# An arena of on-chip places for a streaming encoder step: a new order of handing places out, and two column pairs moved

## The chip, the core and the metric

The kernel runs on one core of a Trainium2 chip. The metric is the device time of one execution in microseconds (us), less being better. Engines are named as the profile names them: PE multiplies matrices and PEld loads its weights, DVE, ACT and POOL work on vectors, SP and POOL (and here and there ACT) issue transfers (DMAs). Each engine works through its own instructions in the order in which the program gives them.

## What is computed

One layer of a hybrid encoder, for 512 rows of a new stream and 32 rows of a running one (544 rows in all, width 2048), everything in fp32:

```python
mod = silu(c) @ w_ada + b_ada                       # shift, scale, gate
h = rmsnorm(x, norm_g) * (1 + scale) + shift
z = h @ w_in                                        # 120 blocks of 128 columns
ya = gelu(au) * (tril(ws) @ rmsnorm(gelu(av)) + bs) * silu(ag)      # 8 groups
yb = rglru(causal_conv(lx)) * silu(lg)                              # 8 blocks
yc = rmsnorm(hgrn2_scan(hq, hf, hi)) * silu(hg)                     # 8 heads
out = (ga * (ya @ wb0) + gb * (yb @ wb1) + gc * (yc @ wb2)) @ w_out # ga, gb, gc: sigmoid(mg)
y = rmsnorm(x + gate * out, final_g)
```

The states of the recurrences and the normalised rows of `av` are outputs too.

## The kernel before

**Stages.** First comes the conditioning and `h` (about the first 130 us). Then the 120 column blocks of `w_in` are multiplied in 60 pairs of columns, one `Group` each; then the three branch products (`merges`), then `w_out` and the final norm. Each matrix product is done with an operand split into a high and a low part, three matmuls for each 128x128 weight block.

**A group.** The rows are cut in two halves of 272 (`HF`), and two column blocks are done in seven products ("items") of 24 matmuls each, in the order `2, 6, -1, 5, -7, 3, 4`, where -1 and -7 are items 1 and 7 of the group that follows. The last group has no group after it, so its items are 2, 6, 5, 3, 4. Items 6, 5 and 3 of a group add up in the same PSUM bank, and ACT copies the bank out between them. The two results stand in places `o1` and `o2`, with half places `u1`, `u2` and `v` on the way. Item 4 calls the group's `post`.

**What runs behind the products.** After every item `pump()` gives one step to each background generator. A step's instructions join the queues of ACT, DVE, POOL and PE behind those of the item. The generators are: `put_away` (writes a finished column block to DRAM, a "spill", with a sigmoid before it for two kinds of columns, into a place `t` of its own), `hg_gen` (one of eight heads after the other, some 36 steps each, during the groups from about 280 to 1190 us), `gm_gen` (eight), `lru_gen` (eight, 12 steps or so each) and `y_gen` (loads spilled branch outputs again and splits them into the operands `X[...]`). Weights come through SP; half of them are added up by DMAs that POOL issues, and POOL also issues the spills and the loads of spilled blocks.

**The order of the groups** is written out in `z_groups`: the four `av` pairs, 14 times a light pair and a pair of head columns (with two head pairs in front), eight light pairs, eight heavy pairs for `gm_gen`, one light pair, eight heavy pairs for `lru_gen`, one light pair. A light pair holds two `mg` blocks, which are only spilled; a heavy pair starts a `gm_gen` or an `lru_gen`. The last pair also starts the two `y_gen` that fill `X[1]` and `X[2]` for the first branch product, one after its item 1 and one after its item 2; each loads eight half blocks through POOL.

**The arena.** All these places are cut from one SBUF tile of 32 units by the class `Arena`, while the program is written, not while it runs. A unit holds 276 numbers in each partition. `get(n)` asks `find(m)` for `m` units in a row: 1 for a half block, 2 for a whole block of 544 columns (16 even pairs of units), 3 for the two `xs` of `hg_gen`, 5 once. `free` marks the units free at that point of the program. An instruction that writes a place waits on the chip until everything that still used the place has ended: the last reader, or the landing of the DMA that spills it. Before, `find(2)` goes round the pairs, from the one after the last it gave out to the next that is free; `find(1)` takes the free unit with the highest number that lies beside a busy one. Which place was freed when has no part in it.

Of the kernel before, what the change touches and what calls it, by code (L numbers as in the profile page):

```python
# [45 lines left out]
class Arena:  # L46
# [3 lines left out]
    def __init__(self, t, units):  # L50
        self.t, self.units = t, units
        self.busy = [False] * units
        self.at = 0

    def find(self, m):
        b = self.busy
        if m == 1:
            for i in reversed(range(self.units)):
                if not b[i] and ((i ^ 1) >= self.units or b[i ^ 1]):
                    return i  # L60
            return next((i for i in reversed(range(self.units)) if not b[i]), None)
        if m == 2:
            n = self.units // 2
            for j in range(n):
                i = 2 * ((self.at + j) % n)
                if not (b[i] or b[i + 1]):
                    self.at = (i // 2 + 1) % n
                    return i
            return None
        return next((i for i in range(self.units - m, -1, -1) if not any(b[i:i + m])), None)  # L70

    def get(self, n):
        m = -(-n // UNIT)
# [10 lines left out]
    def free(self, r):  # L84
        for i in range(r[0], r[0] + r[1]):
            assert self.busy[i]
            self.busy[i] = False


class Buf:  # L90
# [16 lines left out]
def hybrid_step_kernel(ctx: ExitStack, tc: tile.TileContext, xT, cT, w_first, w_in, w_branch, w_out,  # L107
# [61 lines left out]
    def buf(n=T):  # L169
        return Buf(arenas["a"], n)  # L170
# [7 lines left out]
    def P(name, i=0, n=1):  # L178
        o = _POFF[name] + i
        return par[:, o:o + n]  # L180
# [3 lines left out]
    def act(out, in_, func, **kw):  # L184
        if func in (AF.Exp, AF.Ln):
            if table["now"] not in ("exp_ln", "exp_tanh" if func == AF.Exp else None):
                logs()
        elif func not in (AF.Copy, AF.Identity, AF.Square, AF.Relu, AF.Abs):
            table["now"] = "exp_tanh" if func == AF.Tanh else str(func)
        return nc.scalar.activation(out, in_, func, **kw)  # L190
# [51 lines left out]
    def spill(name, n=T, rows=128):  # L242
        scratch[name] = tc.dram_tile([rows, n], F32, name="d_" + name.replace(" ", "_"))
        return scratch[name]
# [202 lines left out]
    def start(gen):  # L447
        bg.append(gen)
# [170 lines left out]
    def av_post(j):  # L619
        def post(*os):  # L620
            for i, o in enumerate(os):
                start(av_gen(j + i, o))
        return post
# [86 lines left out]
    def hg_setup():  # L710

        hg["keep"] = hbuf()
        nc.vector.memset(hg["keep"].ap, 1.0)
        nc.vector.memset(fv(hg["keep"].ap, 0, [[32, T // 32], [1, 1]]), 0.0)
        hg["A"] = hbuf(SLOT)
        nc.gpsimd.memset(hg["A"].ap, 0.0)
        t = hbuf(len(LEVELS) * 256)
        nc.gpsimd.dma_start(out=t.ap, in_=consts[:, 130:130 + len(LEVELS) * 256])
        for _ in range(3):
            yield  # L720
        nc.vector.tensor_copy(masks.rearrange("p a e n -> p (a e n)"), t.ap)
        t.free()
        yield
        d, lb, l1, ln1 = (lbt[:, i, :] for i in range(4))
        x = P("lb", 0, 8)
        tt(d, x, x, op=OP.subtract)
        yield
        act(d, d, AF.Exp)
        yield
        nc.vector.reciprocal(lb, d)  # L730
        tt(lb, lb, d, op=OP.mult)
        tt(lb, lb, lb, op=OP.subtract)
        ts(l1, lb, -1.0, 1.0, op0=OP.mult, op1=OP.add)
        yield
        act(ln1, l1, AF.Ln)
        hg["ready"] = True
# [302 lines left out]
    def lru_setup():  # L1039

        x = P("lam", 0, 8)
        e, u, u2, acc, c8, n8 = (lru_c[:, i, :] for i in range(6))
        ts(e, x, -1.0, None, op0=OP.mult)
        tt(e, e, x, op=OP.min)
        yield
        act(e, e, AF.Exp)
        yield
        ts(u2, e, 2.0, None, op0=OP.add)
        nc.vector.reciprocal(acc, u2)
        tt(u, e, acc, op=OP.mult)  # L1050
        tt(u2, u, u, op=OP.mult)
        nc.vector.memset(acc, 1.0 / 19)
        for n in (17, 15, 13, 11, 9, 7, 5, 3, 1):
            tt(acc, acc, u2, op=OP.mult)
            ts(acc, acc, 1.0 / n, None, op0=OP.add)
            if n % 4 == 3:
                yield
        tt(acc, acc, u, op=OP.mult)
        ts(e, x, -1.0, 0.0, op0=OP.mult, op1=OP.max)
        stt(acc, acc, 2.0, e, op0=OP.mult, op1=OP.add)  # L1060
        ts(c8, acc, -8.0, None, op0=OP.mult)
        ts(n8, acc, 8.0, None, op0=OP.mult)

    def lru_post(b):
        w = []

        def fetch():
            w.append(buf(256))
            nc.gpsimd.dma_start(out=w[0].ap, in_=lru_w[b].rearrange("p a n -> p (a n)"))

        def post(x, lg):
            start(lru_gen(b, x, lg, w[0]))
        return post, fetch
# [68 lines left out]
    def z_groups():  # L1142
        av = [(B_AV + j, B_AV + j + 1, av_post(j)) for j in range(0, 8, 2)]

        def put_away(n, o, on=None):

            yield
            if n[:2] in ("hq", "hg"):
                t = buf()
                act(t.ap, o.ap, AF.Sigmoid)  # L1150
                yield
                if n[:2] == "hq":
                    tt(o.ap, o.ap, t.ap, op=OP.mult)
                else:
                    stt(o.ap, o.ap, P("onorm_g"), t.ap, op0=OP.mult, op1=OP.mult)
                t.free()
            nc.gpsimd.dma_start(out=spill(n), in_=o.ap)
            o.free()
            if on:
                on()  # L1160
            yield

        def keep(*names, on=None):
            def post(*os):
                for n, o in zip(names, os):
                    g = put_away(n, o, on if n == names[-1] else None)
                    start(g)
            return post

        def on_head(h):  # L1170
            def f():
                heads["ready"] = h + 1
            return f

        light = [(B_MG + j, B_MG + j + 1, keep(f"mg {j}", f"mg {j + 1}")) for j in range(0, 48, 2)]
        head = []
        for h in range(8):
            head.append((B_HF + h, B_HQ + h, keep(f"hf {h}", f"hq {h}")))
            head.append((B_HI + h, B_HG + h, keep(f"hi {h}", f"hg {h}", on=on_head(h))))
        heavy = []  # L1180
        for g in range(8):
            cell = {}

            def post(u, sg, cell=cell):
                cell["o"] = (u, sg)
            heavy.append((B_AU + g, B_AG + g, post, lambda g=g, cell=cell: start(gm_gen(g, cell))))
        for b in range(8):
            heavy.append((B_LX + b, B_LG + b, *lru_post(b)))
        todo = av + head[:2]
        todo[4] += ({1: lambda: start(hg_setup())},)  # L1190
        for i in range(14):
            todo += [light[i], head[2 + i]]
        todo += light[14:22]
        todo[-1] += ({1: lambda: start(lru_setup())},)
        rest = iter(light[22:])
        for i, (b1, b2, post, at_start) in enumerate(heavy):
            todo.append((b1, b2, post, {6 if i < 8 else 1: at_start}))
            if i % 8 == 7:
                todo.append(next(rest))
        todo += rest  # L1200
        todo[-1] += ({1: lambda: start(y_gen(0, (1, 2), 0)), 2: lambda: start(y_gen(0, (1, 2), 1))},)
        groups = [Group(n, *t) for n, t in enumerate(todo)]
        groups[0].add(1)
        groups[0].add(7)
        for n, g in enumerate(groups):
            nxt = groups[n + 1] if n + 1 < len(groups) else None
            for i in (2, 6, -1, 5, -7, 3, 4):
                if i > 0:
                    g.add(i)
                elif nxt:  # L1210
                    nxt.add(-i)
# [199 lines left out]

    start_items()
    z_groups()
    merges()
    out_items()
# [112 lines left out]
```

## Time and profile before

| | |
|---|---|
| median of 3 runs | 2116.24 us (2115.29 to 2116.81) |
| profiled execution, own time | 2116.11 us |
| its span, first to last instruction | 2114.4 us |
| granted PE clock, mean over the span | 0.973 of full |
| PE busy | 2005.6 us, 95% of the span |
| DVE, ACT, POOL busy | 61%, 52%, 25% |

The 1.7 us between the own time and the span lie outside the instructions. A busy PE is one with a matmul in flight, so the 95% are not 95% of its peak. A row of a timeline gives the start, the length, the engine, the line of the kernel, the operation and "out<-in"; brackets hold the idle time of the engine before it and what ended that. "arena" stands for any place of the arena, `d_mg`, `d_hi`, `d_y` and the like for spilled blocks in DRAM, `pm` and `pp` for PSUM banks of the groups and of the later products.

### The profile page before, as it was taken

Reading aid. Unit: us, or ns where it says so; the run is one execution under the profiler, and the core shown is the slowest. Engines: PE = TensorE matmul, PEld = TensorE weight load, DVE = VectorE, ACT = ScalarE, POOL = GpSimd, SP = SyncE. Lnnn points to the kernel's source line nnn. Section 1 sums busy time; section 2 is a strip of 40 time slices with the busy share of each in tenths; the row PEclk is TensorE's granted clock in tenths of the full one; section 3 lists DMA queues with packets and bytes.
Section 4 is the critical chain, followed back from the end, with each engine's and each line's share of the span. In section 5 each row is a group of like instructions: output and inputs, shape, how many; then the busy total and the mean of one; then the engine's idle time right before and its main releaser. Section 6 shows DMA issues by size and latency. Waiting matters only on the chain. (4 is left out here: it accounts for less than half of the span.)

```text
span 2114.4 us, 40619 instructions
## 1 busy us (share of the span) xinstructions
PE 2005.6 (95%) x15864; PEld 1912.6 (90%) x15864; DVE 1288.1 (61%) x2204; ACT 1104.0 (52%) x2137; POOL 519.4 (25%) x728
## 2 busy tenths in 40 slices
PE   5779999999998989999999999999989999999997
PEld 2269999999998989999999999999989999999996
DVE  3366666766757666777667677778885333442226
ACT  3457755646655555656555565557765333432223
POOL 0001123232323232332323333212233222211112
PEclk8689999999999999999999999999999999999998
DMA  8977776666666667766777676766666677565554
GB/s 326 351 217 183 199 191 183 194 181 185 191 187 162 173 173 189 196 177 191 202 188 191 190 201 190 193 178 164 173 183 228 221 182 199 185 197 168 171 180 165
DMA packets 134112, 412.21 MB, mean 195 GB/s; under 512 B 16128, under 2 KB 37408, under 8 KB 133920
## 3 DMA queue, kind: packets, MB, share of 16 engines
q1 hardware_dynamic: 86256, 260.55, 37.3%
q0 software_dynamic: 41680, 138.87, 28.3%
q10 hardware_dynamic: 5984, 10.19, 1.5%
q8 instruction: 125, 2.05, 0.4%
q14 instruction: 67, 0.55, 0.1%
HBM read 363.77 MB, written 45.78 MB: 194 GB/s over the span
## 5 line engine op out<-in xcount | busy, mean ns | idle before, releaser
L324 PE MATMUL pm<-x,wh 128*128 128x272 f32 x6720 | 1294.7, 292 | 40.2 <-ACT arena L190 25.0
L324 PEld LDWEIGHTS pm<-x,wh 128*128 128x128 f32 x6720 | 1069.3, 191 | 49.4 <-ACT arena L190 32.2
L324 PE MATMUL pm<-x,wl 128*128 128x272 f32 x3360 | 977.0, 291 | 3.1 <-DVE wl L232 3.0
L232 DVE TENSOR_TENSOR wl<-raw,wh 128x512 fp32r<-128x512 f32 x652 | 467.4, 744 | 361.2 <-ACT wh L190 358.2
L324 PEld LDWEIGHTS pm<-x,wl 128*128 128x128 f32 x3360 | 638.3, 190 | 5.4 <-DVE wl L232 5.4
L190 ACT ACTIVATE wh<-raw 128x512 fp32r<-128x512 f32 x652 | 391.8, 625 | 321.7 <-PE pm L324 204.3
L324 PE MATMUL pp<-x,wh 128*128 128x272 f32 x2560 | 485.9, 289 | 1.3 <-DVE arena L395 1.3
L324 PEld LDWEIGHTS pp<-x,wh 128*128 128x128 f32 x2560 | 400.9, 188 | 15.5 <-issue 15.0
L324 PE MATMUL pp<-x,wl 128*128 128x272 f32 x1280 | 368.7, 288 | 0.1
L232 DVE TENSOR_TENSOR wl<-q,wh 128x512 fp32r<-128x512 f32 x360 | 255.9, 738 | 171.3 <-ACT wh L190 166.6
L190 ACT ACTIVATE wh<-q 128x512 fp32r<-128x512 f32 x360 | 217.0, 626 | 105.3 <-PE pm L324 75.6
L190 ACT ACTIVATE arena<-arena 128x544 f32<-128x544 f32 (+5 forms) x310 | 162.6, 555 | 199.0 <-DMA arena<-d_mg 69.0
L324 PEld LDWEIGHTS pp<-x,wl 128*128 128x128 f32 x1280 | 240.6, 188 | 0.3 <-DVE wl L232 0.3
L190 ACT ACTIVATE arena<-pm 128x272 f32<-128x272 f32 x240 | 94.0, 392 | 167.7 <-PE pm L324 135.7
L266 POOL DMA_DIRECT2D q<-in_w_in_dram x60 | 53.6, 893 | 488.3 <-DMA q<-in_w_in_dram 285.9
L365 DVE TENSOR_TENSOR q<-q,raw 128x1024 f32<-128x1024 f32 x120 | 149.5, 1246 | 4.1
L190 ACT ACT_TABLE_LOAD x59 | 75.7, 1283 | 17.0 <-DMA d_hi<-arena 6.6
L266 POOL DMA_DIRECT2D raw<-in_w_in_dram x60 | 54.4, 907 | 94.1 <-DVE q L365 28.9
L804 POOL TENSOR_TENSOR arena<-arena 128x544 f32<-128x544 f32 (+1 forms) x40 | 55.4, 1417 | 47.5 <-PE px L832 23.7
L1265 DVE TENSOR_TENSOR arena<-pp,arena 128x544 f32<-128x544 f32 x48 | 34.7, 723 | 38.0 <-PE pp L324 38.0
L1372 POOL TENSOR_TENSOR tail<-tail,arena 128x544 f32<-128x544 f32 (+1 forms) x15 | 18.6, 1239 | 150.7 <-ACT arena L190 150.7
L190 ACT ACTIVATE arena<-px 128x128 f32<-128x128 f32 (+4 forms) x136 | 43.4, 332 | 10.5 <-PE px L1309 4.0
(266 smaller groups left out, 1429.9 us busy)
## 6 DMA issues: line engine op xcount, KB each, us to landing
raw<-in_w_in_dram SPq DMA_DIRECT2D x240, 512.0 KB, 4.9
q<-in_w_in_dram SPq DMA_DIRECT2D x60, 512.0 KB, 4.6
q<-in_w_in_dram POOLq DMA_DIRECT2D x60, 512.0 KB, 7.1
raw<-in_w_in_dram POOLq DMA_DIRECT2D x60, 512.0 KB, 7.3
raw<-in_w_branch_dram SPq DMA_DIRECT2D x48, 512.0 KB, 4.1
raw<-in_w_ss_dram SPq DMA_DIRECT2D x44, 512.0 KB, 6.7
raw<-in_w_out_dram SPq DMA_DIRECT2D x38, 512.0 KB, 4.7
raw<-in_w_gate_dram SPq DMA_DIRECT2D x32, 512.0 KB, 4.3
```

Of the source, the lines that this page charges most:

```text
L190: return nc.scalar.activation(out, in_, func, **kw)
L232: tt(lo, src, hi.bitcast(F32), op=OP.subtract)
L266: nc.gpsimd.dma_start(out=raws[n], in_=src, accum_op=OP.add)
L324: mm(p, a, rhs(k, r), start=start and i == 0 and q == 0, stop=stop and i == n - 1 and q == 2, **kw)
L365: tt(raws[n], raws[n], raws[m], op=OP.add)
L804: ptt(v, fv(src, 0, [[2 * m, nb], [m - 1, 2], [1, m]]), fv(src, m - 1, [[2 * m, nb], [0, 2], [0, m]]), op=OP.subtract)
L1265: tt(two(g.ap), halves(p), two(g.ap), op=OP.mult)
L1372: ptt(a[:, n], a[:, n], b.ap[:, n], op=OP.add)
```

## The change

Two edits. `Arena` numbers its frees, and `find` gives out, for one unit, the free unit beside a busy one that was freed first (else any free unit that was freed first); for two, the free pair whose later freed unit was freed first; units never used count as freed at the start. Runs of three and more units are taken from the top as before. And the light pair that stood between the eight `gm_gen` pairs and the eight `lru_gen` pairs now stands behind the latter, in front of the last light pair.

```diff
-        self.at = 0
+        self.last, self.now = [0] * units, 0
     def find(self, m):
-        b = self.busy
+        b, last = self.busy, self.last
         if m == 1:
-            for i in reversed(range(self.units)):
-                if not b[i] and ((i ^ 1) >= self.units or b[i ^ 1]):
-                    return i
-            return next((i for i in reversed(range(self.units)) if not b[i]), None)
+            free = [i for i in range(self.units) if not b[i]]
+            beside = [i for i in free if (i ^ 1) >= self.units or b[i ^ 1]]
+            return min(beside or free, key=lambda i: last[i], default=None)
+        step = 2 if m == 2 else 1
+        free = [i for i in range(0, self.units - m + 1, step) if not any(b[i:i + m])]
         if m == 2:
-            n = self.units // 2
-            for j in range(n):
-                i = 2 * ((self.at + j) % n)
-                if not (b[i] or b[i + 1]):
-                    self.at = (i // 2 + 1) % n
-                    return i
-            return None
-        return next((i for i in range(self.units - m, -1, -1) if not any(b[i:i + m])), None)
+            return min(free, key=lambda i: max(last[i:i + m]), default=None)
+        return free[-1] if free else None
...
             self.busy[i] = False
+            self.now += 1
+            self.last[i] = self.now
...
             todo.append((b1, b2, post, {6 if i < 8 else 1: at_start}))
-            if i % 8 == 7:
-                todo.append(next(rest))
         todo += rest
```

No instruction is added or taken away.

## Rows read from the trace of the kernel before

**Rows 1.** The page's first line.

```profile
span 2114.4 us, 40619 instructions
```

**Rows 2.** Windows: length, busy us (instructions) by engine, granted clock, DMA share, GB/s.

```profile
1360.00:1380.00 20.00, 20.00 (x162) 20.00 (x161) 13.65 (x21) 9.96 (x18) 3.99 (x6) 1.00 0.76 206
...
1540.00:1560.00 20.00, 19.98 (x151) 19.27 (x150) 16.99 (x30) 14.82 (x28) 9.02 (x19) 1.00 0.68 197
```

**Rows 3.** PE's waits, 140 to 1600 us: total us, times, longest.

```profile
PE pm L324 <- ACT arena L190: 25.0, 10, 5.6
PE px L951 <- ACT arena L190: 5.4, 1, 5.4
PE pm L324 <- DVE arena L381: 3.7, 2, 2.5
...
PE pm L324 <- ACT wh L190: 2.5, 2, 1.5
```

**Rows 4.** DMA issues: queue, count, KB each, median us from issue to landing.

```profile
d_mg<-arena POOLq DMA_DIRECT2D x48, 272.0 KB, 6.8
...
d_y<-arena POOLq DMA_DIRECT2D x24, 272.0 KB, 3.3
...
d_hi<-arena POOLq DMA_DIRECT2D x8, 272.0 KB, 6.8
```

**Rows 5.** Timeline around 472 us.

```profile
466.28 0.91 POOL L1157 DMA_DIRECT2D d_hi<-arena  x1
...
474.47 1.28 ACT L190 ACT_TABLE_LOAD   x1 [6.64 <-DMA d_hi<-arena]
...
477.82 0.47 PE L951 MATMUL px<-ident,arena 128*128 128x128 f32 x1 [5.36 <-ACT arena L190]
```

**Rows 6.** Timeline around 757 us.

```profile
758.28 0.66 ACT L190 ACTIVATE arena<-arena 128x544 f32<-128x544 f32 x1 [6.68 <-DMA d_mg<-arena]
...
761.64 0.59 PE L324 MATMUL pm<-x,wh 128*128 128x272 f32 x1 [4.91 <-ACT arena L190]
```

**Rows 7.** Timeline around 653 us.

```profile
652.09 1.16 POOL L804 TENSOR_TENSOR arena<-arena 128x544 f32<-128x544 f32 x1 [2.66 <-DMA d_mg<-arena]
...
654.60 0.39 PE L324 MATMUL pm<-x,wh 128*128 128x272 f32 x1 [1.55 <-ACT wh L190]
```

**Rows 8.** Timeline around 1439 us.

```profile
1435.65 0.75 ACT L190 ACTIVATE arena<-arena,lru_c 128x544 f32<-128x544 f32 x1 [2.95 <-DMA d_y<-arena]
...
1440.53 0.42 PE L324 MATMUL pm<-x,wh 128*128 128x272 f32 x1 [1.78 <-ACT arena L190]
```

**Rows 9.** Windows of PE alone, behind five stalls: PE busy, granted clock, DMA.

```profile
477.80:486.00 8.20, 8.18 (x52) 0.77 0.47 145
654.60:662.60 8.00, 7.79 (x47) 0.79 0.22 72
...
761.60:769.60 8.00, 7.96 (x52) 0.79 0.41 131
1440.50:1448.50 8.00, 7.97 (x51) 0.79 0.67 147
...
1579.50:1587.50 8.00, 8.00 (x47) 0.71 0.55 167
```

**Rows 10.** Timeline from the last group into the first branch product.

```profile
1568.78 0.39 PE L324 MATMUL pm<-x,wh 128*128 128x272 f32 x1 [2.49 <-ACT arena L190]
...
1570.96 0.83 DVE L1092 SCALAR_TENSOR_TENSOR arena<-arena,par 128x32 f32<-128x32 f32 x3
...
1572.32 0.55 POOL L1221 DMA_DIRECT2D arena<-d_y  x1 [6.54 <-issue]
...
1577.05 0.75 ACT L190 ACTIVATE x<-arena 128x272 fp32r<-128x272 f32 x2 [1.45 <-DMA arena<-d_y]
...
1579.49 0.60 PE L324 MATMUL pm<-x,wh 128*128 128x272 f32 x1 [5.61 <-ACT arena L190]
...
1589.12 0.36 PE L324 MATMUL pp<-x,wh 128*128 128x272 f32 x1 [1.28 <-DVE arena L395]
```

## The prediction

> **What bounds the kernel now.** I read the page first, then windows of equal length, then PE's waits, and then the timeline at each of PE's longer stalls. The span is 2114.4 us [rows 1], and in the stage of the groups PE's share is full for long stretches: 162 matmuls in a window of 20 us with PE busy for all of it, while DVE is busy for 13.65 us of it and, in the stretch of `lru_gen`, for 16.99 [rows 2]. So PE sets the time, an item of 24 matmuls takes 24 x 20/162 = 3.0 us, and nothing that shortens another engine's work counts unless PE waits for it. The change takes no work from any engine. What it can give back is PE's idle time and nothing else.
>
> From 140 to 1600 us PE's four largest waits come to 25.0 + 5.4 + 3.7 + 2.5 = 36.6 us [rows 3]. The name in them is mostly ACT, but ACT is the messenger. At 472 us ACT sat idle for 6.64 us in front of a table load, until the spill of a `d_hi` block landed; that spill had been issued at 466.28, and PE then lost 5.36 us [rows 5]. Near 757 ACT sat 6.68 us for a landing `d_mg` and PE lost 4.91 [rows 6]. Near 653 it was POOL that waited 2.66 us for a `d_mg`, ACT behind POOL, and PE lost 1.55 [rows 7]. Near 1439 ACT waited 2.95 us for a `d_y`, and PE lost 1.78 [rows 8]. None of these instructions reads a spilled block. They write a place out of which a block is still being copied: `t` in `put_away`, `t1` of `hg_gen`, its `w32["b"]`, `th` of `lru_gen`. The round of `find(2)` had reached a pair freed one or two pumps earlier.
>
> **The cost of one such stall** is more than its idle time. Behind each the granted clock is down: 0.77 over 8.20 us, and 0.79 over 8.00 us three times [rows 9], a mix of 1.2 and 2.4 GHz after PE had been idle. At clock c a stretch of length L does c x L of the work, so L x (1 - c) is lost: 1.89, 1.68, 1.68 and 1.68 us. The four cost 5.36 + 1.89 = 7.25, 1.55 + 1.68 = 3.23, 4.91 + 1.68 = 6.59 and 1.78 + 1.68 = 3.46 us, together 20.53.
>
> **Part 1, the order of the places.** Which pair is the oldest? I counted places in the code. Of 16 pairs, `hg_gen` holds two throughout (`keep`, `A`) and from three to about eight beside them, and the groups hold two to four. That leaves two to nine free. Some 17 pairs and two triples are asked for in a head's 36 steps and two or three pairs in a group's seven, about 0.9 a pump. A free pair that waits its turn is then two to nine pumps old, 6 to 27 us at 3.0 us an item. A spill lands after a median of 6.8 us for `d_mg` and `d_hi` and 3.3 us for `d_y` [rows 4]. So in order of age nearly every pair is back before it is written again; only at a head's fullest steps, with two or three pairs free, can a wait return. In the stretch of `lru_gen` I count ten pairs held at most, so six are free, and the stall near 1439 should go for certain.
>
> What is late next where such a stall goes? The same steps come once for each of eight heads, and PE waited at L951 for 5.4 us in one of them alone [rows 3]: in the other seven nothing shows behind it. The bounds of this part are 0 (each stall comes back at another step) and 20.53 us. I take all four as gone and one wait of the cheaper kind (3.23 to 3.46, say 3.4) as new: 20.5 - 3.4 = 17.1 us.
>
> A rule of the Trainium skill speaks against this part. "DMA: Bandwidth & Descriptors", in its section on the anatomy of a DMA issued from GpSimd, fits a transfer to about 2.0 us plus its bytes over 436 GB/s. For 128 x 544 x 4 = 278,528 bytes that makes an estimate of 2.6 us, less than one item, so that a place freed a single pump ago would be back; by that rule this part is worth nothing and the sum would be part 2's alone, 2110.2 us. The trace disagrees, with 6.8 us for `d_mg` and 8.2 us from 466.28 to ACT's restart at 474.47 [rows 4, 5].
>
> **Part 2, the light pair.** Where it leaves, between the heavy eights, it covered nothing: PE is busy for 20.00 of 20.00 us there, DVE for 13.65 and ACT for 9.96 [rows 2]. The last `gm_gen` needs five more steps after its pair's last item, and the first `lru_gen` starts only with the last item of its own pair, seven pumps on. I cost this end at nothing, hidden by DVE's free 6 us in 20; without that cover it would be one stall of the 3.46 us kind.
>
> Where it arrives there is something to gain. In the last group PE loses 2.49 us and then 5.61, and 1.28 at the first branch product, with a clock of 0.71 over the 8.00 us after the second (2.32 us lost): 9.38 + 2.32 = 11.70 us [rows 9, 10]. The 5.61 come from `y_gen`: its second eight loads stood on POOL for 6.54 us, and the first went out at 1572.32, just after DVE had ended the three L1092 of the last `lru_gen` at 1571.79. A load does not read what L1092 makes; it most likely writes the half place `xs` that L1092 still read. ACT then waited for the loads, twice, the second time 1.45 us, with the copies out of the bank queued behind [rows 10]. POOL's additions into the weights stand in the same queue. In the changed kernel the last `lru_gen` starts seven items before these loads, its L1092 is long done, and `find(1)` would not give out its `xs` first anyway. Both edits remove the same wait.
>
> What stays: in the last group items 6, 5 and 3 follow each other in one bank, so each waits for ACT's copy, and ACT has sixteen splits at 0.75/2 = 0.37 us, 6 us in all, to do in those items. The 1.28 us at the change of banks stays too. Bounds 0 and 11.70; I take half, 5.9 us, since the 5.61 and its clock are 7.9 of the 11.7 and part of them will turn into the wait for ACT's own work.
>
> **Sum.** 17.1 + 5.9 = 23.0 us off the profiled execution's own 2116.11 (its span and 1.7 us around it; the median is 2116.24) gives 2093.1 us, 1.1% less. About 0.2%, 4.2 us, is what a measurement of this kernel can tell from no change.
>
> **Rivals.** *Too few places, not a bad order.* In the heads' stage the oldest free pair is still too young, or the wait only changes its step. Then 3.46 of part 1 and part 2's 5.9 are left: 2116.1 - 9.4 = 2106.7 us. For it: PE's dearest stalls are in that stage, where I count as few as two free pairs. Against it: the step at L951 stalled in one head of eight, although each head finds the same number of free pairs. The Trainium skill's "Perfetto Trace Analysis" (Optimization Strategy) says that consistent bubbles, the same gap repeating, can mean too little SBUF for the next tile; by that rule a repeating stall would make this rival the forecast, and the trace shows a stall that doesn't repeat.
>
> *Slower: ACT meets more spills.* The new `find(1)` spreads half places over the pairs beside busy ones, fewer whole pairs stay free at the heads' fullest steps, and a pair spilled in one pump is written by ACT in the next. A meeting on ACT cost 7.25 and 6.59 us, 6.9 in the mean; the heads' stage now pays 7.25 + 3.23 + 6.59 = 17.07. With 9.4 gained elsewhere and 4.2 to be seen, it ends slower from 30.7 us on, that is five meetings: 5 x 6.9 - 17.07 - 9.4 = 8.0, so 2124 us. Against it: that is more than one head in two, where now there are two in eight.
>
> *No change to be seen.* The other stalls, 36.6 - 21.7 = 14.9 us (the 21.7 being the four above and the two in the last group [rows 3, 5 to 8, 10]), have to do with ACT, DVE and POOL meeting at the wrong time. PE running earlier shifts these meetings and could double them: 2114 us.
>
> *More than forecast.* Nothing new, and all of part 2: 2116.1 - 32.2 = 2083.9 us.
>
> **How the numbers follow.** Forecast 0.56 (its own range 2086 to 2101), too few places 0.18, more 0.06, no change 0.11, slower 0.09. The range 2081 to 2111 takes in the first three, 0.80, and a little room under 2083.9 for the other stalls to shrink; it leaves out the last two. Below 2112 lie 0.80, within 0.2% 0.11, above 0.09.
>
> **What would show it.** In the trace after, no ACT row that waits for a spill (`d_hi`, `d_mg`, `d_y`) stands before a PE stall; PE's waits for ACT fall from 30.4 us [rows 3] to about 14 (30.4 less 5.36, 4.91, 1.78 and half of 8.1); L1221 doesn't wait on POOL; behind the places named the granted clock stays at 1.00. I am wrong if ACT still waits 6 us for spills in the heads' stage, if POOL's writes of `xs`, still taken from the top, now meet spills, or if the last group loses 9 us again.

## The result, and the profile after

The changed kernel takes 2090.97 us (median of 4 runs, 2088.92 to 2095.28), the kernel before 2115.76 us in the same comparison: a ratio of 0.9887, 95% interval 0.9872 to 0.9901. That is 24.8 us less, where 23.0 had been forecast. The profiled execution has an own time of 2091.84 us. The page's first line answers to [rows 1]:

```profile
span 2090.0 us, 40604 instructions
```

PE's waits from 140 to 1600 us (total us, times, longest) answer to [rows 3]:

```profile
PE pm L322 <- ACT arena L188: 9.2, 7, 3.0
PE pm L322 <- DVE arena L379: 6.2, 5, 2.5
PE pm L322 <- ACT wh L188: 3.7, 2, 2.6
```

Lines are numbered two lower than before (L324 is L322, L190 is L188), and four lower behind the second edit in `z_groups` (L1221 is L1217). PE's waits for ACT's writes of the arena have fallen from 25.0 + 5.4 = 30.4 us to 9.2. The forecast for this was about 14. ACT's own waits in the same stretch hold a row that the kernel before doesn't have, for DVE's L839, and a single short row for a spill of `d_hi`, `d_mg` or `d_y` (before, these made 6.6, 7.1 and 4.2 us):

```profile
ACT arena L188 <- DVE arena L839: 11.3, 4, 4.4
...
ACT arena L188 <- DMA d_mg<-arena: 2.5, 1, 2.5
```

At the place of the dearest stall, near 472 us, the table load in front of `t` begins 0.25 us after the `d_hi` spill is issued, and PE's transpose, which had waited 5.36 us [rows 5], has no wait in its row:

```profile
469.57 0.91 POOL L1155 DMA_DIRECT2D d_hi<-arena  x1
...
469.82 1.28 ACT L188 ACT_TABLE_LOAD   x1
...
474.26 0.38 PE L949 MATMUL px<-ident,arena 128*128 128x128 f32 x2
```

The clock went with it. In windows of PE alone at the four places (length, PE busy, granted clock, DMA share, GB/s), three are at 1.00 now where [rows 9] had 0.77 to 0.79; the one near 650 us is at 0.63:

```profile
474.80:483.00 8.20, 8.20 (x65) 1.00 0.66 182
648.60:656.60 8.00, 5.41 (x23) 0.63 0.21 70
752.00:760.00 8.00, 8.00 (x66) 1.00 0.35 108
...
1430.00:1440.00 10.00, 10.00 (x76) 1.00 0.63 156
```

That one is the stall of [rows 7] in a worse form: POOL waits 5.84 us for a `d_mg`, ACT 4.89 for POOL, PE 2.59 for ACT.

```profile
647.61 2.24 POOL L802 TENSOR_TENSOR arena<-arena 128x544 f32<-128x544 f32 x2 [5.84 <-DMA d_mg<-arena]
...
648.78 0.75 ACT L188 ACTIVATE arena<-arena 128x272 f32<-128x272 f32 x2 [4.89 <-POOL arena L802]
...
651.21 0.82 PE L322 MATMUL pm<-x,wh 128*128 128x272 f32 x2 [2.59 <-ACT wh L188]
```

The last group, against [rows 10] (2.49, 5.61 and 1.28):

```profile
1553.15 0.52 PE L322 MATMUL pm<-x,wh 128*128 128x272 f32 x2 [2.97 <-ACT arena L188]
...
1556.92 0.52 PE L322 MATMUL pm<-x,wh 128*128 128x272 f32 x2 [0.49 <-ACT arena L188]
...
1564.75 0.49 PE L322 MATMUL pp<-x,wh 128*128 128x272 f32 x2 [1.54 <-DVE arena L393]
```

**Where the time went, place by place.** The groups' items are the same number in both traces, so the k-th item's start in the one less its start in the other is PE's lead there, idle time and clock together. The lead grows by 7.3 us near 472, by 5.4 near 684, by 6.6 near 757, by 3.4 near 1439, by 3.0 in small steps of up to 0.8 through the stretch of `lru_gen`, and by 8.9 in the last group. It shrinks by 1.6 before the first item (the conditioning, which the change doesn't touch), 0.3 near 340, 0.9 near 570, 2.0 near 653, 4.2 near 1125, and 1.6 where the light pair used to stand. Small steps near 783 and 1191 add 0.7. Together, before rounding, that is 24.6 us at the last item. The branch products and all behind them take 525.3 us in both traces (from 1589.12 and 1564.75 us to the ends of the spans).

The 1.6 us where the light pair used to stand are no cost. Each of the eight `lru_gen` has eight matmuls of its own between two items, about 1.6 us of PE time. In the kernel before, the first and the last eight run here, the last ones in the last group:

```profile
1401.83 1.99 PE L1102 MATMUL px<-arena 128*128 128x272 f32 x8
...
1571.89 2.00 PE L1102 MATMUL px<-arena 128*128 128x272 f32 x8
```

With the light pair behind them, all eight sets run one group (seven items) earlier, and the last group has none:

```profile
1369.72 2.00 PE L1100 MATMUL px<-arena 128*128 128x272 f32 x8
...
1530.12 2.00 PE L1100 MATMUL px<-arena 128*128 128x272 f32 x8
```

So the lead falls by 1.6 us at the first set, and the same 1.6 us are part of the 8.9 in the last group. The 7.3 us that are left of these are idle time and clock.

Two of the steps had not been foreseen: the gain near 684 and the new stall near 1125. In the kernel before, PE waited near 684 us for 3.39 us behind an ACT copy that itself waited for a POOL instruction:

```profile
681.85 1.23 ACT L190 ACTIVATE arena<-arena 128x544 f32<-128x544 f32 x1 [3.26 <-POOL arena L877]
...
687.58 0.82 PE L324 MATMUL pm<-x,wh 128*128 128x272 f32 x2 [3.39 <-ACT arena L190]
```

In the changed kernel the same copy waits near 1122 us for DVE's writes of `A`:

```profile
1121.28 1.28 DVE L839 COPY_PREDICATED arena<-masks,px 128x128 f32<-128x128 uint8 x6
...
1122.69 3.08 ACT L188 ACTIVATE arena<-arena 128x544 f32<-128x544 f32 x5 [4.38 <-DVE arena L839]
...
1127.14 0.52 PE L322 MATMUL pm<-x,wh 128*128 128x272 f32 x2 [1.96 <-ACT arena L188]
```

The copy is `act(v, k, AF.Copy)` in `lev_w(1)`. It reads `kb` and `qb`, which are two places, through one view with a step of `KO`, the distance between them. It reads neither `A` nor what L877 makes (`ke`). In the changed program `A` lies at unit 8, and `kb` and `qb` lie at units 0 and 10, 0 and 14, 2 and 30, 2 and 26 in heads 0, 1, 6 and 7: `A` is between them in exactly the four heads in which the row counts a wait. In the kernel before `A` lies at unit 0 and is never between. So the copy appears to wait for whoever writes anything from the first to the last unit of its view. I call that the wide view; the experiments test it.

### The profile page after: what moved, and what is told of

Same layout as the page of the kernel before. It is cut to its first block, busy times and chain, and to the rows that moved or that the text cites. A ratio compares the mean times of both kernels' runs of the same rounds, so it can differ in the third digit from the quotient of the medians.

```text
span 2090.0 us, 40604 instructions
## 1 busy us (share of the span) xinstructions
PE 1998.1 (96%) x15864; PEld 1907.2 (91%) x15864; DVE 1284.4 (61%) x2204; ACT 1103.3 (53%) x2136; POOL 527.3 (25%) x728
## 4 chain that ended last, share of the span: by engine, by line
PE 50%; DVE 1%; ACT 1%; issue 0%; DVEq 0%; ACTq 0%
PE pm L322 24%; PE pp L322 23%; PE px L1305 1%; PE px L1100 1%; ACT arena L188 0%; PE px L684 0%; DVE wl L230 0%; PE px L828 0%; ACT wh L188 0%; DVE arena L1404 0%; PE px L1318 0%; PE px L685 0%; DVE arena L839 0%; PE px L920 0%; PE px L980 0%
## 5 line engine op out<-in xcount | busy, mean ns | idle before, releaser
L322 PE MATMUL pm<-x,wh 128*128 128x272 f32 x6720 | 1288.5, 291 | 28.0 <-ACT wh L188 11.1
L322 PEld LDWEIGHTS pm<-x,wh 128*128 128x128 f32 x6720 | 1064.5, 190 | 36.2 <-ACT arena L188 15.3
L322 PE MATMUL pm<-x,wl 128*128 128x272 f32 x3360 | 974.4, 290 | 2.2 <-DVE wl L230 2.2
L230 DVE TENSOR_TENSOR wl<-raw,wh 128x512 fp32r<-128x512 f32 x652 | 461.9, 735 | 361.1 <-ACT wh L188 358.2
L322 PEld LDWEIGHTS pm<-x,wl 128*128 128x128 f32 x3360 | 635.3, 189 | 4.1 <-DVE wl L230 4.0
L188 ACT ACTIVATE wh<-raw 128x512 fp32r<-128x512 f32 x652 | 391.7, 624 | 328.1 <-PE pm L322 196.6
L322 PE MATMUL pp<-x,wh 128*128 128x272 f32 x2560 | 485.9, 289 | 1.5 <-DVE arena L393 1.5
L322 PEld LDWEIGHTS pp<-x,wh 128*128 128x128 f32 x2560 | 400.9, 188 | 15.8 <-issue 15.3
L322 PE MATMUL pp<-x,wl 128*128 128x272 f32 x1280 | 368.6, 288 | 0.0
L230 DVE TENSOR_TENSOR wl<-q,wh 128x512 fp32r<-128x512 f32 x360 | 251.7, 728 | 168.0 <-ACT wh L188 163.1
L188 ACT ACTIVATE wh<-q 128x512 fp32r<-128x512 f32 x360 | 215.9, 626 | 105.3 <-PE pm L322 71.3
L188 ACT ACTIVATE arena<-arena 128x544 f32<-128x544 f32 (+5 forms) x310 | 163.2, 554 | 193.3 <-DVE arena L1358 76.7
L322 PEld LDWEIGHTS pp<-x,wl 128*128 128x128 f32 x1280 | 240.6, 188 | 0.2 <-DVE wl L230 0.2
L188 ACT ACTIVATE arena<-pm 128x272 f32<-128x272 f32 x240 | 94.2, 393 | 153.9 <-PE pm L322 141.2
L188 ACT ACTIVATE arena<-px 128x128 f32<-128x128 f32 (+4 forms) x136 | 43.3, 332 | 7.4 <-PE px L1305 4.0
```

What stands on the lines that cost most here:

```text
L230: tt(lo, src, hi.bitcast(F32), op=OP.subtract)
L322: mm(p, a, rhs(k, r), start=start and i == 0 and q == 0, stop=stop and i == n - 1 and q == 2, **kw)
```

## The experiments

Each was compared with the kernel before on the same chip, whose medians there were 2115.6, 2115.1, 2117.5 and 2116.0 us. The first four split the change.

**The light pair alone.** The kernel before, with only the second edit, which moves one pair of columns:

```diff
-            if i % 8 == 7:
-                todo.append(next(rest))
```

> The kernel before with only the light pair moved; places are given out as before. Theory (the gain of the heads' stage and of the lru stage comes from the order of the places, the wait of the second eight loads in the last group goes with either edit): the stalls near 472, 653, 684, 757 and 1439 us stay as they were, L1221 no longer waits 6.5 us on POOL, and the last group loses about 5 us instead of 9.4: 2108 to 2112 us. Rival (the wait in the last group was one for a place and needs the new order): 2114 to 2117 us, with L1221 still waiting. Rival (the light pair brings most of the 24.8 us): under 2102 us.

Measured 2109.03 us, ratio 0.9968 (0.9955 to 0.998). As expected, in the last group PE's 5.61 us wait is down to 0.49, POOL's second eight loads wait 0.84 us instead of 6.54 [rows 10], and among ACT's waits that for `d_hi` stands as before. The stall near 1439 is there too, one group earlier with its `lru_gen`: ACT waits 2.80 us for a `d_y` at 1416.93.

```profile
ACT L190 <- DMA d_hi<-arena: 6.8, 1, 6.8
```

The last group in its timeline:

```profile
1568.46 2.28 POOL L1219 DMA_DIRECT2D arena<-d_y  x4 [0.84 <-DVE arena L381]
...
1569.71 0.52 PE L324 MATMUL pm<-x,wh 128*128 128x272 f32 x2 [3.10 <-ACT arena L190]
...
1574.99 0.52 PE L324 MATMUL pm<-x,wh 128*128 128x272 f32 x2 [0.49 <-ACT arena L190]
```

**The order of places alone.** The changed kernel, with those two lines put back.

> The changed kernel with the light pair put back between the two heavy eights; only the order of the places is new. Theory: the stalls near 472, 684, 757 and 1439 us are gone, 653 is still there, and in the last group L1221 does not stand behind L1092 either, because the half place xs is no longer the first to be given out: 2094 to 2099 us. Rival (the light pair brings ten us or more): 2104 us or more.

Measured 2095.31 us, ratio 0.9901 (0.9886 to 0.9916). The heads' stage is that of the changed kernel. The last group keeps its long stall: POOL's loads wait twice, 3.76 and 2.22 us, and PE 5.54 us.

```profile
1549.10 0.54 POOL L1219 DMA_DIRECT2D arena<-d_y  x1 [3.76 <-DVE x L230]
...
1550.50 0.83 DVE L1090 SCALAR_TENSOR_TENSOR arena<-arena,par 128x32 f32<-128x32 f32 x3
...
1551.85 3.19 POOL L1219 DMA_DIRECT2D arena<-d_y  x6 [2.22 <-issue]
...
1558.92 0.82 PE L322 MATMUL pm<-x,wh 128*128 128x272 f32 x2 [5.54 <-ACT arena L188]
```

So the time is as expected, but the prediction's sentence that both edits remove the same wait was wrong: the sixteen half places of `y_gen` use up the older ones and reach `xs` of the last `lru_gen` all the same. In this program the third of the second eight loads gets unit 25, which was that `xs`; it goes out 0.52 us after the last L1090 has ended. Only the moved pair spares this wait.

**Half places by age alone.** The changed kernel, with the old round for pairs:

```diff
-        self.last, self.now = [0] * units, 0
+        self.at, self.last, self.now = 0, [0] * units, 0
...
-            return min(free, key=lambda i: max(last[i:i + m]), default=None)
+            n = self.units // 2
+            for j in range(n):
+                i = 2 * ((self.at + j) % n)
+                if not (b[i] or b[i + 1]):
+                    self.at = (i // 2 + 1) % n
+                    return i
+            return None
```

> The changed kernel with the old round for pairs, the new order for half places alone, and the light pair moved. Theory: the heads' stalls come from pairs, so they stay, and ACT is still seen waiting about 6 us for d_hi and d_mg ahead of PE stalls there; the half places by age spare DVE and ACT the waits in the stretch of lru_gen, which are worth 1 to 4 us to PE. With the light pair's 6.6 us: 2105 to 2110 us. Rival: the half places by age carry the heads' gain too, since they decide which pairs stay whole; then 2092 to 2100 us and the waits of ACT for d_hi and d_mg are gone. Second rival: half places by age break up more pairs and the old round meets more spills, 2112 us or more.

Measured 2102.70 us, ratio 0.9939 (0.9922 to 0.9955), between the theory and the first rival. The theory's rows are there: ACT waits for `d_hi` and `d_mg`, and PE behind them. In the stretch of `lru_gen` ACT's waits for DVE's L1092, 23.3 us in 6 times before, have no row left. The stalls near 650 and 684 are gone too; there the lead over the kernel before grows by 3.6 and 4.8 us. Beside the light pair alone (0.9968) the half places are worth some 6 us, more than the 1 to 4 that I expected, and in another stage.

```profile
473.29 1.28 ACT L194 ACT_TABLE_LOAD   x1 [5.47 <-DMA d_hi<-arena]
...
748.85 1.20 ACT L194 ACTIVATE arena<-arena 128x544 f32<-128x544 f32 x2 [6.18 <-DMA d_mg<-arena]
...
752.20 0.82 PE L328 MATMUL pm<-x,wh 128*128 128x272 f32 x2 [5.11 <-ACT arena L194]
```

**Pairs by age alone.** The changed kernel, with the old `find(1)`, from the top:

```diff
-            free = [i for i in range(self.units) if not b[i]]
-            beside = [i for i in free if (i ^ 1) >= self.units or b[i ^ 1]]
-            return min(beside or free, key=lambda i: last[i], default=None)
+            for i in reversed(range(self.units)):
+                if not b[i] and ((i ^ 1) >= self.units or b[i ^ 1]):
+                    return i
+            return next((i for i in reversed(range(self.units)) if not b[i]), None)
```

> The changed kernel with the choice of half places as before (highest free unit beside a busy one); whole pairs go by age. Theory (the stalls were waits for whole pairs, spilled or still read; half places cost PE nothing): the stalls near 472, 684, 757 and 1439 us stay away, ACT's waits for L1092 (23.3 us before) come back without a PE stall behind them, 2089 to 2096 us. Rival (half places carry part of the gain, by waits for u1 or xs): 2098 us or more, with PE stalls behind L1092 or L381.

Measured 2094.71 us, ratio 0.9904 (0.989 to 0.9919). The time is in the expected range, but not by the expected road: the heads' stage is some 9 us better than in the changed kernel (no stalls near 650 and 1125), and late in `lru_gen` a half place whose block was just being spilled gives it back:

```profile
1534.42 0.40 ACT L189 ACTIVATE arena<-pm 128x272 f32<-128x272 f32 x1 [8.32 <-DMA d_y<-arena]
...
1534.87 0.82 PE L323 MATMUL pm<-x,wh 128*128 128x272 f32 x2 [5.45 <-ACT arena L189]
```

**The newest pair first.** If the age of a place is what counts, the opposite order must cost much:

```diff
-            return min(free, key=lambda i: max(last[i:i + m]), default=None)
+            return max(free, key=lambda i: max(last[i:i + m]), default=None)
```

> The changed kernel, but find(2) gives out the pair that was freed last in place of the one freed first. Theory (what counts is how old a pair is when it is written again): ACT, DVE and POOL wait for spills and late readers in every head and in every lru block, with 5 to 7 us lost for each meeting on ACT; with two or more in each of sixteen of them over 100 us: 2200 us or more. Rival (such waits were two or three unlucky meetings, and engines mostly have slack): under 2150 us.

Measured 2295.36 us, ratio 1.086 (1.0845 to 1.0875): 180 us more. ACT's waits for spills, over 140 to 1600 us:

```profile
ACT L188 <- DMA d_hi<-arena: 51.3, 7, 9.8
...
ACT L188 <- DMA d_hf<-arena: 48.1, 7, 10.1
...
ACT arena L188 <- DMA d_y<-arena: 18.5, 5, 5.4
```

Seven heads of eight now pay what one paid before. By the rule of the Trainium skill ("DMA: Bandwidth & Descriptors", anatomy of a DMA issued from GpSimd) a spill of this size would be an estimated 2.6 us and age would not matter; the row of 51.3 us in 7 waits, 7.3 each, disagrees.

**Two copies, one for each place.** This takes the wide view away and leaves the places where they are:

```diff
-                act(v, k, AF.Copy)
+                for o, s in ((0, 0), (gap + m, KO + m)):
+                    act(fv(x, o, [[2, nb], [1, 1]]), fv(kb.ap, s, [[2, nb], [1, 1]]), AF.Copy)
```

> The changed kernel; the ACT copy of lev_w(1), whose one view runs from kb to qb, is made as two copies, each inside its own place. In heads 0, 1, 6 and 7 of the changed kernel the place of A lies between kb and qb, and in these four heads alone this copy waited for DVE's writes of A (L839, 11.3 us in all). Theory (a wait through the view's span): the four waits of ACT for L839 go, the stall near 1125 us goes, 2085 to 2089 us. Rival (the copy was merely late for another reason, such as the small DVE operations of lru_setup, in the queue before L839): the waits stay and the time is within 1.5 us of the changed kernel's 2091.

In the changed kernel: 2082.42 us, ratio 0.9843 (0.983 to 0.9857), 8.5 us under it and somewhat better than expected. ACT's row for L839 and the stall near 1125 are gone. Of the lead that this kernel has over the changed one, 4.2 us come near 1125, and 1.5 stand before the first item, where the edit does nothing.

> The kernel before with one edit: the copy of the kept carry states in lev_w(1) is made by two ACT instructions, one for each of the two places, instead of one instruction whose view spans from the one place to the other. Theory (the wide view): what the two copies gained behind the change, 8.5 us, came from the writes of A that lay between the two places in four heads. In the kernel before A lies at unit 0 and never between them, so nothing is gained here: 2113 to 2118 us, and no row in which ACT waits for the writes of A, before or after the edit. Rival: two copies are better in themselves (shorter ones, or a better meeting of ACT and DVE); then they gain here too, 2106 to 2110 us.

In the kernel before: 2112.31 us, ratio 0.998 (0.9971 to 0.9989). A gain where the theory gave none: I had looked for `A` between the places and not for others. The copy near 682 us waited there for POOL's `ke`, which lies at unit 6, between `kb` at 2 and `qb` at 24; in the other seven heads of this kernel `ke` lies outside. As two copies it runs without a wait, and PE's stall behind it is gone; near 684 the lead grows by 6.2 us, the rest of the trace moving by less than 2 at any place.

```profile
681.22 0.79 ACT L190 ACTIVATE arena<-arena 128x272 f32<-128x272 f32 x2
```

But two copies together take 0.79 us where the one took 1.23, so they might also be better in themselves. That is the next pair.

**Two copies cut by columns.** Two instructions of half the length, each with a view that still spans both places:

```diff
-                act(v, k, AF.Copy)
+                for o in (0, nb):
+                    act(fv(x, o, [[2, nb // 2], [gap + m, 2], [1, m]]),
+                        fv(kb.ap, o, [[2, nb // 2], [KO + m, 2], [1, m]]), AF.Copy)
```

> The changed kernel with the copy of lev_w(1) cut in two by columns, not by places: two ACT instructions of half the length, each with a view that still spans from the one place to the other. This keeps the wide view and gives the shorter instructions. Theory (the wide view): ACT still waits some 11 us for the writes of A in four heads and PE stalls near 1125 us, so the time stays that of the changed kernel, 2088 to 2094 us (ratio 0.987 to 0.990). Rival (shorter copies are better in themselves): 2081 to 2085 us as with one copy for each place (ratio 0.983 to 0.986). In between: both.

> The kernel before with the same cut by columns. In the kernel before one copy, near 682 us, waits 3.26 us for POOL's writes of a place that lies between, with a PE stall of 3.39 us behind it; with one copy for each place both were gone and 5.2 us gained. Theory (the wide view): cut by columns the wait and the stall stay, and nothing is gained: ratio 0.998 to 1.002. Rival (shorter copies): ratio 0.996 to 0.998 as before, with the stall gone although the view still spans both places.

Behind the change: 2090.19 us, ratio 0.9878 (0.9863 to 0.9893), the changed kernel's time. In the kernel before: 2117.36 us, ratio 1.0001 (0.9992 to 1.001). Both as the theory had it. The waits stay, first those behind the change, then the one in the kernel before with PE's stall:

```profile
ACT arena L188 <- DVE arena L841: 11.2, 4, 3.8
```

```profile
685.83 1.48 ACT L190 ACTIVATE arena<-arena 128x272 f32<-128x272 f32 x2 [2.22 <-POOL arena L879]
...
691.81 0.40 PE L324 MATMUL pm<-x,wh 128*128 128x272 f32 x1 [3.02 <-ACT arena L190]
```

**Runs of three by age too.** The stall near 650 should be `xs`, a run of three units, still taken from the top:

```diff
-        if m == 2:
+        if m in (2, 3):
```

> The changed kernel, with runs of three units (xs of hg_gen) also taken by age in place of from the top. Theory (the stall near 650 us, which the change left, is POOL's first write of xs in a run at the top that was just spilled): the 5.6 us wait of POOL at L802 for d_mg and PE's 2.59 us behind it are gone, 2085 to 2088 us. Rival (another place is written there, or a run of three is never old): the wait stays or moves to another head, 2089 to 2094 us.

Measured 2094.23 us, ratio 0.9897 (0.9883 to 0.991), not the gain that was expected. POOL's wait fell from 5.84 us to 3.24 and PE's from 2.59 to 2.12, but all places moved, and `A` now lies between `kb` and `qb` in six heads, 0 to 5. ACT waits for L839 near 679 and 792, and PE loses 4.19 and 3.00 us behind these:

```profile
649.87 1.15 POOL L802 TENSOR_TENSOR arena<-arena 128x544 f32<-128x544 f32 x1 [3.24 <-DMA d_mg<-arena]
...
678.89 1.22 ACT L188 ACTIVATE arena<-arena 128x544 f32<-128x544 f32 x1 [3.71 <-DVE arena L839]
...
684.61 0.52 PE L322 MATMUL pm<-x,wh 128*128 128x272 f32 x2 [4.19 <-ACT arena L188]
```

**Both of these, age for all runs and two copies.**

> The two copies together with runs of three by age. Theory (runs by age cost time only because other pairs then put A between kb and qb in heads that had it outside, and POOL's wait at the first writes of xs does get shorter): the ACT waits for L839 that came back near 680 and 795 us go, 2077 to 2081 us, under the 2082.4 of the two copies alone. Rival (runs by age break up pairs and shorten every other place's rest): 2084 us or more.

Measured 2079.0 us, ratio 0.983 (0.9817 to 0.9844), the best of all and as expected: no row for L839, POOL's wait near 643 at 2.02 us. It is 12.0 us under the changed kernel. Against the two copies alone the 95% intervals overlap.

```profile
643.14 1.16 POOL L802 TENSOR_TENSOR arena<-arena 128x544 f32<-128x544 f32 x1 [2.02 <-DMA d_mg<-arena]
```

**The loads of the last group through SP.** In the changed kernel's last group ACT waits 2.26 us for weights whose addition stands on POOL behind the first eight loads. On top of the two copies, the sixteen loads go through SP:

```diff
-                nc.gpsimd.dma_start(out=b.ap, in_=s if h is None else s[:, h * HF:(h + 1) * HF])
+                (nc.gpsimd if h is None else nc.sync).dma_start(out=b.ap, in_=s if h is None else s[:, h * HF:(h + 1) * HF])
```

> The two copies, and the sixteen loads of the y_gen that fill X[1] and X[2] issued by SP in place of POOL. Theory (in the last group of the changed kernel ACT waits 2.26 us for an addition into weights that stands on POOL behind eight loads of 0.54 us each): that wait goes, PE's 2.48 and 1.70 us in the last group fall by half or more, 2077 to 2080 us. Rival (ACT's sixteen splits and the copies out of one bank set the pace there, or SP's weights come late behind the loads): 2081 to 2086 us.

Measured 2085.22 us, ratio 0.9857 (0.9843 to 0.987), no better than the two copies alone. The first wait fell to 0.49 us, the second rose to 4.88, since ACT now waits for the loads themselves. POOL's queue was not all that holds this group up; what else does is left open.

```profile
1544.04 1.59 ACT L188 ACTIVATE x<-arena 128x272 fp32r<-128x272 f32 x4 [4.59 <-DMA arena<-d_y]
...
1547.01 0.60 PE L322 MATMUL pm<-x,wh 128*128 128x272 f32 x2 [4.88 <-ACT arena L188]
```

More places, the direct test of the rival "too few places", were not tried: an arena of 34 units doesn't fit into what is left of the memory.

## Why the prediction was right, step by step

**That PE's idle time and its clock are all there is to gain: right.** PE's waits fell, no engine's work did, and the branch products took 525.3 us in both.

**The price of a stall (idle time plus lost clock): right.** Near 472 7.25 us was worked out and 7.3 came; near 757 6.59 and 6.6; near 1439 3.46 and 3.4.

**The stall near 653: the cause was misread.** I named `w32["b"]`, a pair, and counted 3.23 us as gained. What POOL writes there is the first level of `xs`, a run of three that the change leaves at the top; 2.0 us were lost. My text named just this as a way to be wrong (POOL's writes of `xs` meeting spills), without seeing that it was the stall already counted. Age for runs of three shortened the wait at this line, 5.84 to 3.24 and, with the two copies, to 2.02 us.

**"One wait of the cheaper kind as new", 3.4 us: the size was near, the kind wrong.** The new stall near 1125 costs 4.2 us. It is no spill that isn't back, but the wide view over `A`. Not counted either was its twin before the change, near 684, whose going gave 5.4 us: it stood among the other 14.9 us, and I had not followed it. Both are shown by the two ways of dividing the copy: one copy for each place removes wait and stall, two copies by columns don't. In sum the heads' stage gave 12.6 us (the lead at 1191 us, 11.0, without the 1.6 of the conditioning) where 7.25 + 3.23 + 6.59 - 3.4 = 13.7 had been forecast, out of partly other pieces. That is luck in part.

**The half places: left out.** My 17.1 us spoke of pairs alone. Half places by age are worth some 6 us by themselves, at the stalls near 650 and 684; why these two go with half places is not shown. The places are one pool, so the parts don't add: with the light pair, half places alone gave 0.9939, pairs alone 0.9904, both 0.9887.

**The stretch of `lru_gen`: a term that the sum lacks.** Beyond the stall near 1439 the lead grows by 3.0 us in small steps. No single part of the change owns them: the same growth is in the traces of the light pair alone, the order of places alone, half places alone and pairs alone. What it is made of stays open.

**The light pair: right in kind, under-sized.** 5.9 us were taken; 7.3 came in the last group beside the 1.6 of matmuls that left it, and 6.8 us by itself (0.32% of 2116). The end that the pair leaves, put at nothing, costs nothing: the 1.6 us of lead lost there are the eight matmuls that now come a group earlier. The same step of 1.6 us stands in the light pair alone, and with the order of places alone it is absent.

**"Both edits remove the same wait": wrong**, as the order of places alone shows. It cost the sum nothing, since it was counted once.

**The total: in part luck.** 23.0 us were forecast and 24.8 measured, but the heads' stage gave less than its terms (12.6 for 13.7), the stretch of `lru_gen` more (6.4 for 3.46) and the last group more (7.3 for 5.9), and 1.6 us went in the conditioning.

**The rivals.** Too few places (2106.7 us) fell: the two dear stalls are gone. The slower rival asked for five meetings of ACT with spills in the heads' stage, and none that stands before a PE stall is left; the newest first shows what such meetings cost when they come. No change (2114 us) fell too: the meetings of engines that the lead shifted didn't double; the dearest that went gave 5.4 us (near 684), the dearest that came cost 4.2 (near 1125). Half of what "more than forecast" (2083.9 us) asked, all of part 2, didn't come: 5.00 us of idle time stay in the last group (2.97 + 0.49 + 1.54). The rule by which age would be worth nothing (2110.2 us) fell with the order of places alone, 2095.31 us.

## What to carry to other kernels

Where one pool serves on-chip places and spills read out of it, give out the place that has been free longest; for pairs the opposite order cost 180 us here, while this order of places gave 20. For runs of three it gained nothing by itself (2094.23 against 2090.97 us), since all other places moved with them. Before explaining a wait by the data, list who writes the memory between the first and the last element of the waiting instruction's view: a view that spans two places waits for what lies between, and moving places moves such waits about, which can hide what an edit is worth. A stall whose releaser isn't read by the waiting instruction is to be followed up before it is counted as noise. And a step in the lead is a cost only if no work moved across it: compare what runs between the items before calling it one.

## What was not expected of the hardware and its program

One view over two places made ACT wait 11.3 us in four heads for writes of a third place that it doesn't touch; with one view for each place there was no such wait, and the stall of 4.2 us near 1125 was gone. The wait is the program's, not the chip's: in the program built from the changed kernel, the copy waits on a semaphore for L839 in heads 0, 1, 6 and 7 and in no other; in the one with two copies, none of the sixteen does.

And two copies of 128x272 with one step each took 0.79 us together, where one of 128x544 with two steps took 1.23. Two of 128x272 with two steps took 1.48 in the row shown, where the second waited for the first. One by one, in all eight heads, those with one step took 0.43 to 0.45 us and those of the same size with two steps 0.70 to 0.74: ACT's time hangs on the shape of the view, not only on the count of elements. The shorter time isn't what the two copies gained: in the kernel before it came in all eight heads, and the lead grew by more than 2 us only where the wait had been.
